# The mixer's list schedule given measured durations, and its weights' low parts always made by VectorE

## The chip, the cores and the metric

One core of one Trainium2 chip. The metric is the device time of one execution in microseconds (us). The engines are named as the profile names them: PE is TensorE's matrix multiplication and PEld its loading of weights, DVE is VectorE, ACT is ScalarE, POOL is GpSimd, and SP is SyncE, which here only issues transfers (DMA).

## What is computed

1024 tokens of width 1024 in float32 go through a layer of two kinds of attention, a layer of attention with forgetting, and a last block: the hybrid mixer, attention over a memory of 256 tokens, and a grouped mixture of experts. The change concerns the mixer and, at its two ends, what is handed over to attention over the memory.

```python
def hybrid_mixer(x, w_in, b_i, b_f, conv_qk, head_norm_g, pool_w, pool_scale, w_out):
    z = x @ w_in
    qk = jax.nn.silu(causal_depthwise_conv(z[..., :2 * M], conv_qk))
    q = qk[..., :M].reshape(B, S, H, dh)
    k = qk[..., M:].reshape(B, S, H, dh)
...
    h = mlstm_chunkwise(q, k, v, i_pre, f_pre)
    mu = h.mean(-1, keepdims=True)
    var = jnp.square(h - mu).mean(-1, keepdims=True)
    h = (h - mu) * lax.rsqrt(var + LN_EPS) * head_norm_g.reshape(H, dh).astype(jnp.float32)
    h = h.reshape(B, S, M) * jax.nn.sigmoid(o_pre.astype(jnp.float32))
    pooled = multiscale_pool(u)
    pm = jnp.einsum('bsgc,gcd->bsgd', pooled, pool_w.astype(jnp.float32))
    pm = pm.reshape(B, S, POOL_WIDTH) * pool_scale.astype(jnp.float32)
    mixed = jnp.concatenate([h, pm], axis=-1).astype(x.dtype)
    return mixed @ w_out
...
        mix = hybrid_mixer(x, ...)
        x = layer_norm(DEEPNORM_ALPHA * x + mix, ln_mix_g[l], ln_mix_b[l])
        xa = memory_cross_attention(x, mem, w_xq[l], w_xkv[l], w_xo[l])
```

H is 4 heads, dh is 128, M is 512; the recurrence of a head runs over chunks, and the pooled part has 4 groups of 128 columns.

## The kernel before

A product of two float32 matrices is made as three products of parts. Each operand is split into a high part, a copy that ACT writes in a type of fewer bits (names in h: `wh`, `fh`), and a low part, the operand minus the high part (`wl`, `fl`). `mm3` (L338 to L343) issues the three matmuls: L340 high by high, L341 and L342 high by low. A weight tile is loaded by SP, ACT makes its high part (L316), and its low part is one subtraction of 128x1024 elements (L318).

The mixer (L1380) has the following stages.

- Eight projections `proj` (L1534), two for each of the four heads, of 48 matmuls each, in two halves and four groups of 6; ACT copies a half out of PSUM (L1548); then the convolution: one first tap (L1556), by DVE or POOL, three more taps by DVE (L1552), a tanh by ACT (L1567), and their product by DVE (L1569).
- Four heads `head` (L1576): masks of exponents (`top`, L1602), their exponentials, scores (L1591) weighed by DVE (L1611), keys turned by PE (L1596), the state's matmuls (L1632) and its updates by DVE (L1642, L1644), the numerator (L1660, L1662, ACT's copy L1667), its statistics (L1672 to L1680), the denominator (L1684 to L1687, a power on POOL L1734, L1735), normalising by ACT, the gate (L1695), a transposition (L1700), high and low parts (L1703, L1707).
- `pool_out` (L1743): four loads of the pooled input (L1752), eight matmuls L1756, their parts (L1759, L1763).
- What is left of the products of weights that depend on the memory alone, which cross-attention needs (`Memory.parts`, L1934). Sixteen groups of the first kind (matmuls L1930, ACT and DVE to tiles `kvw` by L1952, stored to `wkd` by L1962) make the score weights; sixteen of the second kind (L1933, copies L1942 and L1950, stored to `vwd` by L1958) the value weights. They load `x_wq`, `x_wo` (L244) and `kvd` (L1873).
- The eight weights of the out-projection (`m_wo`, L280), and the first half of six of its eight output tiles: `y` loaded with the residual (L1801), four groups of 6 matmuls, and the addition by DVE (L1812).

All that is one list schedule. `class Plan` (L504) takes operations with an engine, a cost in us, a key, what they depend on and what room they take and free (slots of SBUF, banks of PSUM). `run` takes again and again the operation that can start first by these costs, and among equals the lower key; it reckons latencies between engines (L39, 4.0 us for a load). If the engine is a pair such as `("dve", "pool")`, with a pair of costs, it takes the one that would end first. It emits the operations in that order, and each engine then executes its own in order, waiting only for what they need. So costs never change what is done, only the order and, for pairs, the engine.

Behind the list, without a list, follows the rest of the out-projection (L428): 24 matmuls for each remaining half tile, the addition (L422), LayerNorm's statistics (L385, L387), its two passes (L394, L395) with gain and bias loaded at L399, and the store of the tile, which cross-attention loads again as `xl` (L1992), turns, and splits (L2011). Its weights `kw` are loaded from `wkd` (L1987) by SP ahead of LayerNorm's gain and bias for the first ten, and behind for the other six.

Of the kernel before, what the change touches and what calls it, by code (L numbers as in the profile page):

```python
# [14 lines left out]
AF = mybir.ActivationFunctionType  # L15
# [1364 lines left out]
def mixer(k, ft, res, before_out, after_tile):  # L1380
# [58 lines left out]
    act, dve = (lambda n: 0.07 + 0.0008 * n), (lambda n: 0.13 + 0.00092 * n)  # L1439
# [81 lines left out]
    def w_ops(i, key, deps, slot):  # L1521

        def load():
            k.late.discard(i)
            k.w_load(i + 1)
        got, steps = {}, k.w_steps(i)
        loaded[0] = plan.op("sp", 0.1, key, load, [loaded[0], *deps], ["w"])
        d = loaded[1] = plan.op("act", 0.95, key, lambda: next(steps), [loaded[0], loaded[1]], ["sl"] * 2 + ["sl?"] * MX_SPARE[1] if slot else ["wl"])

        def sub(e):  # L1530
            got[0] = steps.send((V, nc.gpsimd)[e])
        return got, plan.op(("dve", "pool"), (1.14, 2.3), key, sub, [d], free=["w"])

    def proj(h, j):  # L1534
# [23 lines left out]
        for half in range(2):  # L1558
            for g in range(4):
                d = plan.op("pe", 1.3, key, lambda half=half, g=g: mm(half, g), [d, e] if half else [d],  # L1560
# [3 lines left out]
        d = plan.op(("dve", "pool"), (0.7, 1.05), key, tap3, [e], ["sl"])  # L1564
        for t in (2, 1, 0):
            d = plan.op("dve", 1.2, key, lambda t=t: tap(t), [d])
        d = plan.op("act", 0.95, key, lambda: nc.scalar.activation(z[0], qk[c], AF.Tanh, scale=0.5), [d])  # L1567
        last_proj.append(e)
        return plan.op("dve", 1.2, key, lambda: V.scalar_tensor_tensor(qk[c], z[0], 1.0, qk[c], op0=OP.add, op1=OP.mult), [d], free=["x"])  # L1569
# [6 lines left out]
    def head(h, ready, begin):  # L1576
# [134 lines left out]
        for b in range(2):  # L1711
            t = chain([("dve", 4 * 0.27, call(top, b), ["sl"] if b == 0 else [], ["x"] if b else []),
                       ("act", 4 * 0.29, call(exps, b))], key, [d])
            s = plan.op("pe", 0.64, key, call(scores, b), ready, ["ps"])
            ev.append(plan.op("dve", 0.6, key, call(weigh, b), [s, t], free=["ps"]))
            kt.append(chain([("pe", 0.44, call(turn_k, b), ["pt"]), ("act", 4 * 0.25, call(scale_k, b), ["sl"] if b == 0 else [], ["pt"])],
# [11 lines left out]
        for i, (a, b) in enumerate(groups):  # L1728
            x = plan.op("pe", (b - a) * 0.23, key, call(num_mm, a, b), [P[(b - 1) // 4], P[0], C[i]], [MX_BANKS[3], "ps"] + ["sl"] * (a == 0),
                        ["sl"] * (4 if b == 8 else 0))  # L1730
            x = plan.op("act", act((b - a) * 129), key, call(num_copy, a, b), [x], [], [MX_BANKS[3]])
            x = plan.op("dve", (b - a) * 0.27, key, call(num_add, a, b), [x, w], free=["ps"])
            N.append(plan.op("dve", (b - a) * 0.28, key, call(stats, a, b), [x]))
        d = chain([("dve", 0.4, den), ("pool", 1.65, lambda: nc.gpsimd.tensor_tensor(rs, rs, k.mhalf[:, :8], op=OP.pow)),  # L1734
                   ("dve", 0.1, lambda: V.scalar_tensor_tensor(nmr, mv[:, :, 0], -1.0, rs, op0=OP.mult, op1=OP.mult))], key, N)  # L1735
        for b in range(2):
            done[b, h] = chain([("act", 1.6, call(normal, b), (), ["sl"] if b else []), ("dve", 0.6, call(gate, b)),
                                ("pe", 0.44, call(turn_p, b), ["pt"], ["sl"] * (2 * b)),
                                ("act", act(512), call(hi, b), ["sl"] * (2 if h % 2 == 0 else 0)),
                                ("dve", 0.6, call(lo, b), (), ["pt"])], key, [d] + ([done[b, h - 1]] if h % 2 else []))  # L1740
    done = {}

    def pool_out():  # L1743
# [21 lines left out]
        for g in range(4):  # L1765
            key = MX_KEYS[0] + g / 10
            d = plan.op("sp", 0.1, key, lambda g=g: load(g), [d], ["x"] + ["sl"] * (g == 0))
            for half in range(2):
                d = plan.op("pe", 0.86, key, lambda g=g, half=half: mm(g, half), [d], [MX_BANKS[4]],
                            (["x"] if half else []) + (["sl"] if half and g == 3 else []))  # L1770
                e = plan.op("act", 0.5, key, lambda g=g, half=half: hi(g, half), [d], ["sl"] * (2 if g % 2 == 0 else 0))
                d = done[half, 4 + g] = plan.op("dve", 0.62, key, lambda g=g, half=half: lo(g, half), [e], free=[MX_BANKS[4]])
# [1166 lines left out]
```

## Time and profile before

| what | before |
|---|---|
| median of 3 runs | 2295.5 us (2295.07 to 2298.74) |
| the profiled execution | 2301.81 us, span 2300.0 us |
| its mean granted clock of TensorE | 0.988 |
| PE busy | 2211.1 us, 96% of the span, 12164 instructions |
| DVE busy | 1184.4 us, 51%, 2892 instructions |
| ACT busy | 960.0 us, 42%, 2018 instructions |
| POOL busy | 452.6 us, 20%, 620 instructions |
| DMA | 282.06 MB, mean 123 GB/s |

The profiled execution is one run of its own, and its 2301.81 us contain the span and 1.8 us around it. The share of an engine's busy time is a mean over all stages. The mixer's list covers some 190 us before 1642 us of the span.

### The profile page before, as it was taken

What the parts mean: (1) busy time and instruction counts of PE and PEld (TensorE: products, weight loads), DVE (VectorE), ACT (ScalarE), POOL (GpSimd) and SP (SyncE); (2) the same over time, 40 slices, a digit from 0 to 9 for tenths busy, and PEclk for the clock granted to TensorE, in tenths of its full rate; (3) what the DMA queues carried; (4) which work ended last, traced back from release to release, by engine and by line L of the source; (5) the groups of instructions that cost most, each with busy time, mean ns of one, the idle gap of its engine ahead of it and who ended that gap; (6) DMA issues with size and microseconds to landing.
All of it is one profiled execution on the core that took longest, in us unless ns stands there. A gap on an engine that the chain in (4) does not pass through costs nothing.

```text
span 2300.0 us, 32867 instructions
## 1 busy us (share of the span) xinstructions
PE 2211.1 (96%) x12164; PEld 1757.5 (76%) x12164; DVE 1184.4 (51%) x2892; ACT 960.0 (42%) x2018; POOL 452.6 (20%) x620
## 2 busy tenths in 40 slices
PE   7999999999999999999999999999899999899797
PEld 7888778888877777777788789787577888666564
DVE  6322678834344443444344332687445637766544
ACT  5322667823344444444442221355202122557453
POOL 2000455400122222222310010121001102222121
PEclk9999999999999999999999999999999999999898
DMA  4112221233222211221254221326656124778774
GB/s 165 37 48 99 81 58 38 75 118 104 75 69 72 63 55 60 74 60 56 83 174 147 103 91 47 106 69 216 233 220 259 69 106 176 263 235 293 226 216 165
DMA packets 96515, 282.06 MB, mean 123 GB/s; under 512 B 11980, under 2 KB 25036, under 8 KB 96352
## 3 DMA queue, kind: packets, MB, share of 16 engines
q1 hardware_dynamic: 75616, 225.32, 28.4%
q0 software_dynamic: 6624, 24.12, 4.4%
q10 hardware_dynamic: 14112, 30.48, 4.2%
q8 instruction: 97, 1.59, 0.3%
q14 instruction: 66, 0.54, 0.1%
HBM read 202.73 MB, written 65.62 MB: 117 GB/s over the span
## 4 chain that ended last, share of the span: by engine, by line
PE 85%; DVE 6%; DMA 4%; ACT 3%; issue 2%; SPq 0%; POOL 0%; ACTq 0%; POOLq 0%; DVEq 0%
PE pd L340 15%; PE pd L342 15%; PE pd L341 15%; PE ps L340 4%; PE po L644 4%; PE ps L342 4%; PE ps L341 4%; PE ps L595 3%; PE pt L622 3%; PE pd L2538 2%; PE pd L1902 2%; PE ps L990 2%; PE po L1033 1%; PE pt L1019 1%; PE ps L2562 1%
## 5 line engine op out<-in xcount | busy, mean ns | idle before, releaser
L340 PE MATMUL pd<-fh,wh 128*128 128x512 f32 x880 | 353.5, 402 | 0.6 <-DVE st L1246 0.3
L342 PE MATMUL pd<-fh,wl 128*128 128x512 f32 x880 | 347.9, 395 | 0.5 <-DVE wl L318 0.5
L341 PE MATMUL pd<-fl,wh 128*128 128x512 f32 x880 | 347.4, 395 | 0.0
L340 PE MATMUL pd<-wh,fh 128*128 128x258 f32 (+3 forms) x616 | 203.2, 330 | 2.4 <-DVE n L1436 2.4
L342 PE MATMUL pd<-wh,fl 128*128 128x258 f32 (+3 forms) x616 | 200.9, 326 | 0.0
L341 PE MATMUL pd<-wl,fh 128*128 128x258 f32 (+3 forms) x616 | 200.8, 326 | 0.0
L340 PEld LDWEIGHTS pd<-fh,wh 128*128 128x128 f32 x880 | 165.2, 188 | 43.0 <-issue 7.1
L342 PEld LDWEIGHTS pd<-fh,wl 128*128 128x128 f32 x880 | 165.2, 188 | 40.1 <-issue 2.3
L341 PEld LDWEIGHTS pd<-fl,wh 128*128 128x128 f32 x880 | 165.5, 188 | 34.9 <-issue 0.2
L318 DVE TENSOR_TENSOR wl<-w,wh 128x1024 fp32r<-128x1024 f32 (+5 forms) x92 | 106.8, 1166 | 138.3 <-ACT wh L316 138.3
L316 ACT CAST wh<-w 128x1024 fp32r<-128x1024 f32 (+5 forms) x99 | 97.3, 989 | 139.3 <-PE pd L341 108.2
L630 ACT COPY PT<-pt 128x512 f32<-128x512 f32 (+2 forms) x192 | 86.4, 478 | 139.9 <-PE pt L622 139.4
L609 POOL TENSOR_SCALAR P<-P,rinv 128x256 f32<-128x256 f32 (+7 forms) x128 | 96.1, 751 | 192.3 <-DVE rinv L608 163.3
L606 ACT ACTIVATE P<-P,m 128x256 f32<-128x256 f32 (+7 forms) x128 | 99.6, 778 | 76.7 <-DVE m L600 75.8
L340 PEld LDWEIGHTS pd<-wh,fh 128*128 128x128 f32 x616 | 116.4, 189 | 14.2 <-DVE n L1436 2.8
L341 PEld LDWEIGHTS pd<-wl,fh 128*128 128x128 f32 x616 | 116.3, 189 | 10.6 <-issue 1.0
L342 PEld LDWEIGHTS pd<-wh,fl 128*128 128x128 f32 x616 | 116.3, 189 | 10.2 <-issue 0.2
L1309 POOL TENSOR_TENSOR dm<-lcb,mask 128x128 f32<-128x128 f32 x128 | 60.7, 474 | 282.4 <-DVE m L600 226.3
L595 PE MATMUL ps<-st,st 128*128 128x512 f32 (+3 forms) x384 | 106.9, 372 | 1.2 <-DMA st<-st 0.8
L644 PE MATMUL po<-PT,V 128*64 128x256 f32 (+1 forms) x640 | 96.4, 373 | 0.0
L2420 DVE TENSOR_TENSOR ml<-mw,mh 128x1024 fp32r<-128x1024 f32 x66 | 80.1, 1226 | 29.8 <-ACT mh L2417 15.4
L622 PE MATMUL pt<-ident,P 128*128 128x128 f32 x576 | 88.7, 276 | 2.6 <-POOL P L609 2.4
(513 smaller groups left out, 4721.9 us busy)
## 6 DMA issues: line engine op xcount, KB each, us to landing
mw<-w_moe SPq DMA_DIRECT2D x70, 512.0 KB
w<-o_wc SPq DMA_DIRECT2D x30, 512.0 KB
w<-w_moe SPq DMA_DIRECT2D x26, 512.0 KB
xr<-xs SPq DMA_DIRECT2D x18, 512.0 KB
s<-x_wkv SPq DMA_DIRECT2D x16, 512.0 KB
lcb<-dn SPq DMA_DIRECT2D x16, 512.0 KB
st<-st ACTq DMA_DIRECT2D x64, 128.0 KB
wkd<-kvw SPq DMA_DIRECT2D x32, 256.0 KB
```

The lines of the kernel that those rows point to most:

```text
L316: nc.scalar.copy(hi[:, :n], raw[:, :n])
L318: (eng or nc.vector).tensor_sub(lo[:, :n], raw[:, :n], hi[:, :n].bitcast(F32))
L340: first = mm(out, lhs[0], rhs[0], start=start, stop=False)
L341: mm(out, lhs[0], rhs[1], start=False, stop=False)
L342: mm(out, lhs[1], rhs[0], start=False, stop=stop)
L595: ins = nc.tensor.matmul(ps[:, :m], l, r, start=t == 0, stop=t == len(passes) - 1)
L606: nc.scalar.activation(sb[:, :w], sb[:, :w], AF.Exp, bias=acc, scale=-1.0, accum_out=sm)
L609: nc.gpsimd.tensor_scalar(sb[:, :w], sb[:, :w], ri, 0.0, op0=OP.mult, op1=OP.add)
L622: ins = nc.tensor.transpose(pt[:, j * 128:(j + 1) * 128], p[:, (c + j) * 128:(c + j + 1) * 128], k.ident)
L630: nc.scalar.copy(dst, src)
L644: st["V", n + i] = nc.tensor.matmul(o[a * 64:(a + 1) * 64, cols], val(a, j), PT[i // 2, a, j // 4][:, j % 4, n0:], start=j == 0, stop=j == ...
L2420: nc.vector.tensor_sub(W[c][1], raw[c], W[c][0].bitcast(F32))
```

## The change

Every cost of the mixer's list is replaced by another number; so are the costs of the memory steps. The low part of a weight is no longer given to DVE or POOL, whichever would end first, but always to DVE. Nothing else is changed: the operations, the tiles and the room are the same. These lines show the kinds of edits; the other costs change in the same way.

```diff
-    act, dve = (lambda n: 0.07 + 0.0008 * n), (lambda n: 0.13 + 0.00092 * n)
+    act, dve = (lambda n: 0.155 + 0.00085 * n), (lambda n: 0.155 + 0.00104 * n)
...
-        def sub(e):
-            got[0] = steps.send((V, nc.gpsimd)[e])
-        return got, plan.op(("dve", "pool"), (1.14, 2.3), key, sub, [d], free=["w"])
+        def sub():
+            got[0] = steps.send(V)
+        return got, plan.op("dve", 1.23, key, sub, [d], free=["w"])
...
-                d = plan.op("pe", 1.3, key, lambda half=half, g=g: mm(half, g), [d, e] if half else [d],
+                d = plan.op("pe", 1.4, key, lambda half=half, g=g: mm(half, g), [d, e] if half else [d],
...
-        d = plan.op(("dve", "pool"), (0.7, 1.05), key, tap3, [e], ["sl"])
+        d = plan.op(("dve", "pool"), (0.75, 1.13), key, tap3, [e], ["sl"])
...
-            t = chain([("dve", 4 * 0.27, call(top, b), ["sl"] if b == 0 else [], ["x"] if b else []),
+            t = chain([("dve", 4 * 0.49, call(top, b), ["sl"] if b == 0 else [], ["x"] if b else []),
...
-            x = plan.op("pe", (b - a) * 0.23, key, call(num_mm, a, b), [P[(b - 1) // 4], P[0], C[i]], [MX_BANKS[3], "ps"] + ["sl"] * (a == 0),
+            x = plan.op("pe", (b - a) * 0.45, key, call(num_mm, a, b), [P[(b - 1) // 4], P[0], C[i]], [MX_BANKS[3], "ps"] + ["sl"] * (a == 0),
...
-                @add("act", 0.3 if kind else 0.5)
+                @add("act", 0.37 if kind else 0.6)
...
-                @add("dve", 0.35 if kind else 0.6)
+                @add("dve", 0.42 if kind else 0.68)
```

In all, the seven low parts that POOL made leave it, and the first taps on POOL become four of eight instead of two; no instruction is added or removed. Three places show how the order moves. In the names, the number behind a name only tells tiles apart.

The first place is DVE in the fourth head, from the weighing of its scores on. L318 rows are the low parts of weights of the out-projection, L1642 and L1644 the head's state, L1952 the memory's score weights, L1763 the pooled part. Before:

```order
L1569 SCALAR_TENSOR_TENSOR qk_15025<-z_14902,qk_15025 128x1024
L1952 SCALAR_TENSOR_TENSOR kvw_15048<-ps_15017,kvw_15048 128x512
L1952 SCALAR_TENSOR_TENSOR kvw_15051<-po_15042,kvw_15051 128x512
L1763 SCALAR_TENSOR_TENSOR fl_15095<-ps_15056,psc_13831,fh_15094 128x512
L318 TENSOR_TENSOR wl_15104<-w_15035,wh_15103 128x1024
L1611 SCALAR_TENSOR_TENSOR e_15061<-ps_15108,e_15061 128x512
L1952 SCALAR_TENSOR_TENSOR kvw_15138<-ps_15066,kvw_15138 128x512
L1611 SCALAR_TENSOR_TENSOR e_15061<-ps_15133,e_15061 128x512
L1642 COPY C_15164<-pd_15144 128x129
L1644 SCALAR_TENSOR_TENSOR C_15164<-C_15164,n_12840,pd_15144 128x129 x2
L1626 TENSOR_TENSOR n_12840<-n_12840 128x8
L1627 TENSOR_TENSOR n_12840<-n_12840 128x8
```

Now:

```order
L1611 SCALAR_TENSOR_TENSOR e_15025<-ps_15061,e_15025 128x512
L318 TENSOR_TENSOR wl_15059<-w_14995,wh_15058 128x1024
L1763 SCALAR_TENSOR_TENSOR fl_15067<-ps_15018,psc_13831,fh_15066 128x512
L1611 SCALAR_TENSOR_TENSOR e_15025<-ps_15089,e_15025 128x512
L1626 TENSOR_TENSOR n_12840<-n_12840 128x8
L1627 TENSOR_TENSOR n_12840<-n_12840 128x8
L318 TENSOR_TENSOR wl_15075<-w_14997,wh_15074 128x1024
L1952 SCALAR_TENSOR_TENSOR kvw_15005<-po_14981,kvw_15005 128x512
L1642 COPY C_15132<-pd_15116 128x129
L1644 SCALAR_TENSOR_TENSOR C_15132<-C_15132,n_12840,pd_15116 128x129 x2
L1719 TENSOR_SCALAR n_12840<-n_12840 128x8
L318 TENSOR_TENSOR wl_15145<-w_15100,wh_15144 128x1024
```

Three low parts now stand in DVE's queue from the first weighing to the middle of the state's updates, where one stood ahead of the weighing; two more of that stretch were POOL's. Of three of the memory's L1952 there, one is left.

The second place is SP at the boundary to cross-attention, the last rows ahead of the weights `kw`: stores `vwd` of the memory's value weights, loads of `x_wo` (named s) and `kvd`, and residuals `xr`. Before:

```order
L1801 DMA y_15474<-xs_5683 128x1024
L1958 DMA vwd<-vwo_15472 128x512
L244 DMA s_15504<-x_wo 128x1024
L1873 DMA kv_15506<-kvd 128x2x256
L244 DMA s_15531<-x_wo 128x1024
L1958 DMA vwd<-vwo_15634 128x512
L1958 DMA vwd<-vwo_15641 128x512
L1958 DMA vwd<-vwo_15648 128x512
L1958 DMA vwd<-vwo_15655 128x512
L1826 DMA xr_15660<-xs_5683 128x1024
L1826 DMA xr_15662<-xs_5683 128x1024
L1987 DMA kw_15664<-wkd 128x1024
```

Now:

```order
L1958 DMA vwd<-vwo_15614 128x512
L244 DMA s_15621<-x_wo 128x1024
L1873 DMA kv_15623<-kvd 128x2x256
L1958 DMA vwd<-vwo_15625 128x512
L1958 DMA vwd<-vwo_15635 128x512
L1958 DMA vwd<-vwo_15639 128x512
L244 DMA s_15643<-x_wo 128x1024
L1958 DMA vwd<-vwo_15651 128x512
L1958 DMA vwd<-vwo_15655 128x512
L1826 DMA xr_15660<-xs_5683 128x1024
L1826 DMA xr_15662<-xs_5683 128x1024
L1987 DMA kw_15664<-wkd 128x1024
```

Behind the last `y` load, nine stores of value weights instead of five now stand ahead of the `kw` loads (the first four of the nine are not shown), with a further load of `kvd` and one more of `x_wo`; on PE, eight of sixteen groups L1933 instead of four stand inside the out-projection, the last of them 164 matmuls ahead of its end.

The third place is DVE in the LayerNorm behind the out-projection: the first pass (L394) and the second (L395) of the six tiles `y`, among the additions (L422) of later tiles, `xr` being tile 6. Before:

```order
L387 BN_AGGR mv_15828<-bn_15825 128x2
L394 SCALAR_TENSOR_TENSOR y_15420<-y_15420,mv_15717,s_15684 128x1024
L394 SCALAR_TENSOR_TENSOR y_15422<-y_15422,mv_15754,s_15684 128x1024
L394 SCALAR_TENSOR_TENSOR y_15424<-y_15424,mv_15791,s_15684 128x1024
L394 SCALAR_TENSOR_TENSOR y_15454<-y_15454,mv_15828,s_15684 128x1024
L422 SCALAR_TENSOR_TENSOR y_15470<-y_15470,pd_15836 128x512
L395 SCALAR_TENSOR_TENSOR y_15420<-y_15420,rstd_15719,s_15686 128x1024
L395 SCALAR_TENSOR_TENSOR y_15422<-y_15422,rstd_15756,s_15686 128x1024
L395 SCALAR_TENSOR_TENSOR y_15424<-y_15424,rstd_15793,s_15686 128x1024
L395 SCALAR_TENSOR_TENSOR y_15454<-y_15454,rstd_15830,s_15686 128x1024
L385 BN_STATS bn_15862<-y_15470 128x6
L422 SCALAR_TENSOR_TENSOR y_15474<-y_15474,pd_15885 128x512
```

Now:

```order
L422 SCALAR_TENSOR_TENSOR xr_15660<-xr_15660,ps_15922 128x512
L385 BN_STATS bn_15974<-xr_15660 128x6
L394 SCALAR_TENSOR_TENSOR y_15388<-y_15388,mv_15717,s_15684 128x1024
L394 SCALAR_TENSOR_TENSOR y_15390<-y_15390,mv_15754,s_15684 128x1024
L394 SCALAR_TENSOR_TENSOR y_15392<-y_15392,mv_15791,s_15684 128x1024
L394 SCALAR_TENSOR_TENSOR y_15419<-y_15419,mv_15828,s_15684 128x1024
L394 SCALAR_TENSOR_TENSOR y_15428<-y_15428,mv_15865,s_15684 128x1024
L394 SCALAR_TENSOR_TENSOR y_15432<-y_15432,mv_15914,s_15684 128x1024
L395 SCALAR_TENSOR_TENSOR y_15388<-y_15388,rstd_15719,s_15686 128x1024
L395 SCALAR_TENSOR_TENSOR y_15390<-y_15390,rstd_15756,s_15686 128x1024
L422 SCALAR_TENSOR_TENSOR xr_15660<-xr_15660,pd_15948 128x512
L395 SCALAR_TENSOR_TENSOR y_15392<-y_15392,rstd_15793,s_15686 128x1024
```

Before, four tiles' first passes stood ahead of the fifth tile's addition, and their second passes behind it. Now six first passes stand in one block behind the addition of the first half of tile 6.

## Rows read from the trace of the kernel before

**Rows 1.** Windows: us, then each engine's busy us (instructions), PE's granted clock, DMA share, GB/s.
```profile
1448.00:1580.60 132.60, 131.38 (x700) 111.69 (x699) 99.66 (x243) 60.57 (x135) 25.05 (x10) 1.00 0.32 100
1580.60:1642.60 62.00, 51.30 (x204) 31.91 (x203) 42.12 (x97) 32.51 (x67) 7.42 (x3) 0.97 0.93 328
1642.60:1738.60 96.00, 96.00 (x400) 74.73 (x399) 41.59 (x58) 2.55 (x6) 9.26 (x17) 1.00 0.53 195
1738.60:1790.00 51.40, 49.87 (x242) 40.42 (x241) 29.97 (x49) 21.11 (x46) 0.74 (x2) 1.00 0.63 237
1650.00:1670.00 20.00, 20.00 (x86) 15.95 (x85) 4.90 (x7) 0.69 (x1) 0.00 (x0) 1.00 0.01 2
```

**Rows 2.** Waits of PE, 1448 to 1643: what it waited for, us in all, times, longest.
```profile
PE ps L1930 <- DMA kv<-kvd: 3.0, 1, 3.0
...
PE pt L1700 <- DVE p L1695: 0.9, 1, 0.9
...
PE ps L1591 <- DVE qk L1569: 0.3, 1, 0.3
```

**Rows 3.** Timeline of POOL: start, us, engine, line, operation, tiles, count, idle time before and what ended it.
```profile
1511.90 3.38 POOL L318 TENSOR_TENSOR wl<-w,wh 128x1024 fp32r<-128x1024 f32 x1 [4.99 <-PE pt L1700]
...
1596.30 2.37 POOL L318 TENSOR_TENSOR wl<-w,wh 128x1024 fp32r<-128x1024 f32 x1 [7.55 <-ACT wh L316]
```

**Rows 4.** Timeline of DVE, 1460 to 1645.
```profile
1462.60 5.93 DVE L1552 SCALAR_TENSOR_TENSOR qk<-z,conv,qk 128x1023 f32<-128x1023 f32 x3
...
1512.97 0.68 DVE L1707 TENSOR_TENSOR fl<-pt,fh 128x512 fp32r<-128x512 f32 x1
...
1582.63 3.91 DVE L1552 SCALAR_TENSOR_TENSOR qk<-z,conv,qk 128x1023 f32<-128x1023 f32 x3
1586.46 2.44 DVE L1602 CUSTOM_DVE_ANT_0 e<-ab,mask,n 128x128 f32<-128x128 f32 x1
...
1588.83 0.34 DVE L1602 CUSTOM_DVE_ANT_0 e<-ab,mask,n 128x128 f32<-128x128 f32 x1
...
1630.53 1.23 DVE L318 TENSOR_TENSOR wl<-w,wh 128x1024 fp32r<-128x1024 f32 x1 [1.42 <-ACT wh L316]
```

**Rows 5.** Timeline of PE from the last projection matmul to the out-projection's resumption.
```profile
1580.55 0.60 PE L1700 MATMUL pt<-ident,p 128*128 128x128 f32 x4
1580.98 1.89 PE L1930 MATMUL ps<-kv,s 128*128 128x256 f32 x8
1582.71 1.89 PE L1930 MATMUL po<-kv,s 128*128 128x256 f32 x8
...
1640.37 1.13 PE L1756 MATMUL ps<-pl,s 128*128 128x512 f32 x2 [2.02 <-DMA pl<-pooled]
...
1642.64 0.79 PE L340 MATMUL pd<-wh,fh 128*128 128x512 f32 x1
```

**Rows 6.** Timeline of SP: DMA issues of the tail and the boundary.
```profile
1631.45 0.32 SPq L1752 DMA_DIRECT2D pl<-pooled  x1
...
1689.15 13.34 SPq L1987 DMA_DIRECT2D kw<-wkd  x10
1702.58 0.38 SPq L399 DMA_DIRECT2D s<-ln_mix_g  x1
...
1724.31 1.03 SPq L1992 DMA_DIRECT2D xl<-xs  x2
```

**Rows 7.** Timeline of DVE, 1660 to 1750.
```profile
1710.13 4.87 DVE L394 SCALAR_TENSOR_TENSOR y<-y,mv,s 128x1024 f32<-128x1024 f32 x4 [3.28 <-DMA s<-ln_mix_g]
...
1715.52 4.86 DVE L395 SCALAR_TENSOR_TENSOR y<-y,rstd,s 128x1024 f32<-128x1024 f32 x4
...
1721.92 0.69 DVE L422 SCALAR_TENSOR_TENSOR xr<-xr,ps 128x512 f32<-128x512 f32 x1 [0.35 <-PE ps L342]
...
1739.97 0.67 DVE L2011 TENSOR_TENSOR xl<-pt,xh 128x512 fp32r<-128x512 f32 x1
```

**Rows 8.** The tile kw: operations with durations in ns and first and last start.
```profile
L340 PE MATMUL ps<-kw,xh x16: 391/394/477, 1741.8 to 1752.3; 128*128 128x512 f32 x16
```

More of the change, by code (lines that the diff above doesn't have):

```diff
@@ L1711, in head @@
         for b in range(2):
-            t = chain([("dve", 4 * 0.27, call(top, b), ["sl"] if b == 0 else [], ["x"] if b else []),
[L1713 to L1716, printed above, removed]
+            t = chain([("dve", 4 * 0.49, call(top, b), ["sl"] if b == 0 else [], ["x"] if b else []),
+                       ("act", 4 * 0.39, call(exps, b))], key, [d])
+            s = plan.op("pe", 0.9, key, call(scores, b), ready, ["ps"])
+            ev.append(plan.op("dve", 0.68, key, call(weigh, b), [s, t], free=["ps"]))
+            kt.append(chain([("pe", 0.46, call(turn_k, b), ["pt"]), ("act", 4 * 0.37, call(scale_k, b), ["sl"] if b == 0 else [], ["pt"])],
                             key, ready + [gates]))
@@ L1721, in head @@
         for a, b in ((0, 3), (3, 6), (6, 7)):
-            C.append(chain([("pe", (b - a) * 0.11, call(state_mm, a, b), [MX_BANKS[2]] + ["sl"] * (a == 0), ["sl"] if b == 7 else []),
-                            ("dve", (b - a) * 0.27, call(state, a, b), [], [MX_BANKS[2]])], key,
+            C.append(chain([("pe", (b - a) * 0.224, call(state_mm, a, b), [MX_BANKS[2]] + ["sl"] * (a == 0), ["sl"] if b == 7 else []),
+                            ("dve", (b - a) * 0.345, call(state, a, b), [], [MX_BANKS[2]])], key,
                            [kt[(b - 1) // 4], kt[0]] + C[-1:]))
@@ L1770, in pool_out @@
                             (["x"] if half else []) + (["sl"] if half and g == 3 else []))
-                e = plan.op("act", 0.5, key, lambda g=g, half=half: hi(g, half), [d], ["sl"] * (2 if g % 2 == 0 else 0))
-                d = done[half, 4 + g] = plan.op("dve", 0.62, key, lambda g=g, half=half: lo(g, half), [e], free=[MX_BANKS[4]])
+                e = plan.op("act", 0.68, key, lambda g=g, half=half: hi(g, half), [d], ["sl"] * (2 if g % 2 == 0 else 0))
+                d = done[half, 4 + g] = plan.op("dve", 0.75, key, lambda g=g, half=half: lo(g, half), [e], free=[MX_BANKS[4]])
     for h in range(4):
@@ L1816, in mixer @@
         for j, g in enumerate(MO_ORDER[:4]):
-            d = plan.op("pe", 1.3, key, lambda i=i, g=g: out_part(i, g), [d, y, ready[g], done[0, 2 * g], done[0, 2 * g + 1]],
+            d = plan.op("pe", 1.4, key, lambda i=i, g=g: out_part(i, g), [d, y, ready[g], done[0, 2 * g], done[0, 2 * g + 1]],
                         [bank] if j == 0 else [])
-        plan.op("dve", 0.62, key, lambda i=i: out_add(i), [d], free=[bank])
+        plan.op("dve", 0.69, key, lambda i=i: out_add(i), [d], free=[bank])
     with k.tc.manual_schedule(engines=SW_MAN):
```

18 lines of the change are left out of this document (9 added, 9 removed).

## The prediction

> **What bounds the kernel now.** Read first the windows by stage around the mixer's planned part [rows 1]. PE is busy 131.38 of 132.60 us while the eight projections run, 51.30 of 62.00 in the tail behind them, 96.00 of 96.00 in the rest of the out-projection, and 49.87 of 51.40 where cross-attention begins. So only two stretches can give anything: the tail, where PE idles 10.7 us with its transfers at a share of 0.93 and 328 GB/s, and the boundary. Where PE is full, only work that enters or leaves counts. The PE waits of the planned part come second [rows 2]: the longest, 3.0 us, ends on the load of kvd, and on VectorE (DVE) end 0.9 and 0.3 us while the projections run. Then each engine's timeline: POOL for what a low part costs there [rows 3], DVE for what it costs others [rows 4], PE for where the projections end and the out-projection resumes [rows 5], SP for the loads behind it [rows 6], and DVE and PE at the boundary [rows 7, 8].
>
> Call P the last projection matmul (ended by 1580.55), R the resumption of the out-projection (1642.64) [rows 5], and E its end (1738.60). The list decides P, R and what PE still has to do behind R.
>
> **The low parts.** Seven of sixteen go from POOL, where one alone takes 2.37 us [rows 3], to DVE, at 1.23 us [rows 4]: 7 x 1.23 = 8.6 us more. While POOL made them, DVE's own instructions were stretched in six of seven cases: three taps took 5.93 us instead of 3.91 in the first, one exponent's mask 2.44 instead of 0.34 in the last [rows 4]. The six together add about 11.5 us (six times 1.5 to 2.2). An instruction that reads PSUM was not stretched (L1707, 0.68 us from 1512.97, beside POOL's low part of 1511.90 to 1515.28) [rows 3, 4]. So DVE gets some 3 us lighter; two first taps (L1556) that move to POOL as well are counted at nothing, since no PE wait of the tail ends on them. On the path lie only the 0.9 and 0.3 us that PE waited for DVE [rows 2]: **-1.2 us**, bounds -1.2 and 0; I take all of it, and +0.5 for new waits of the same kind, since low parts now stand in the queue ahead of the gate (L1695).
>
> The Trainium skill, "SBUF — State Buffer", section "SBUF: two separate sides", says that the pair of ports that VectorE and GpSimd share is locked for a whole instruction, and that the other engine waits it out (VectorE where it reads two operands from SBUF). By that rule all seven low parts would give DVE back up to their whole length; the rows give less than that for each, and since neither lies on the path the sum is the same by both.
>
> **P.** The new order has one group of memory weights (L1930) fewer ahead of the last projection matmul and one transposition of head 2 (L1700) fewer. A group is a row of eight matmuls, and the next group starts 1.73 us on, from 1580.98 to 1582.71; the transposition before it holds PE 0.43 us, from 1580.55 to 1580.98 [rows 5]. So P moves by -1.73 - 0.43 - 1.2 + 0.5 = **-2.9 us**.
>
> **The tail, P to R, 62.1 us before.** PE's work in it was 51.3; one L1930 and one L1700 enter (+2.2), four groups of L1933, which I price as L1930's, leave for behind R (12 of 16 stood ahead of it, now 8), 4 x 1.73 = 6.9. That leaves 46.6, so PE is not what ends it: transfers are. R needs the last of the four pooled loads, issued at 1631.45 and waited for until 1640.37 [rows 5, 6], so 8.9 us in flight. In the new order 1.75 MB fewer stand ahead of it: two x_wo loads of 128x1024 in float32 (0.5 MB each), two vwd stores and, since P, one wkd store (0.25 MB each). Two bounds. If the transfers alone set it, 1.75 MB / 328 GB/s = 5.3 us are gained. If the chain of head 3 sets it, less: its product (L1569) has four masks fewer ahead of it (4 x 0.27), no stretch (2.1), but a gate and a low part of 0.69 and 0.68 more, so the scores come some 1.6 us earlier behind P; from there the third low part stands in DVE's queue and waits for its load, I put 2.2 us, and everything behind it, the head's state above all, stands too; slots come free later, and of the 1.6 us little but the time in flight remains. I take 1.6 earlier in issue and 2.1 us shorter in flight (8.9 to 6.8, by the fewer stores ahead), **-3.7 us**, between -5.3 and 0. R: -2.9 - 3.7 = -6.6.
>
> **R to E.** 16 half tiles of 24 matmuls, 6 already done, are 15.75 halves. 86 matmuls take 20.00 us [rows 1], so one takes 0.233 and a half 5.58: 87.9; four L1933 groups add 6.9, and cross-attention's first transpositions the rest of the 96.0. Now eight groups stand there: **+6.9 us**. PE is full, so all of it counts. E: -6.6 + 6.9 = +0.3. What the tail gains is what was carried out of it.
>
> **The boundary.** The last vwd store can go only when the last L1933 is done, and the 16 kw loads stand behind it on SP. Before, SP came to the kw at 1689.15, E - 49.5 [rows 6]. Now the last L1933 stands 164 matmuls ahead of E, 164 x 0.233 = 38.1 us, so the kw start at about E - 36. LayerNorm's gain and bias stand behind the first ten. They were issued 13.4 us behind the first kw, and DVE's first normalising (L394) began 7.5 us after the gain's issue at 1702.58, E - 28.5 [rows 6, 7]. In the new DVE order six L394 stand in one block, behind the first half of tile 6, which ended its add at 1722.61, E - 16 [rows 7]; so the block starts at about E - 15.3. Six L394 at 1.217 (four took 4.87) and the first L395, 8.5 us, make tile 0 ready at E - 6.8. It is stored and read back (xl); before, 7.6 us lay between its normalising (1715.52 + 4.86 / 4 for its L395) and SP's xl at 1724.31, with six kw loads between, so 0 to 7.6; I take 2.9, because the kw are gone by then. DVE meanwhile has five more L395, the adds and statistics of tiles 6 and 7, and reaches cross-attention's first low part (L2011, 1739.97 before, E + 1.4) at about E + 3.3, and one L394 later the second one, until some E + 5.9. The first score matmuls came at 1741.8, E + 3.2 [rows 8], and now come at E + 6.4: **+3.2 us**. Bounds: -1.5, all the idle time of that stretch [rows 1], and +7, if gain and bias land only at E - 11.6.
>
> One row speaks for hiding part of it: from 1650 to 1670 the DMA share was 0.01 [rows 1], so the four stores that leave the tail find free engines there.
>
> **Sum.** -2.9 - 3.7 + 6.9 + 3.2 = **+3.5 us**. Against the profiled execution, 2301.8 us, that is 2305.3. It stood 6.3 us above the median of the three runs, 2295.5; I carry the difference over: **2299.0 us**. About 0.2%, 4.6 us, is what a measurement of this kernel tells from no change, so 2290.9 and 2300.1 are the borders, and the forecast lies inside, near the upper.
>
> **Rivals.**
> Faster (A). The loads no longer stand behind slots in the tail. 20.3 MB went through it (62.0 us at 328 GB/s); less 1.75 are 18.6, and at a share of 1.00 in place of 0.93 (353 GB/s) they need 52.7 us. Then P to R shrinks by 9.4 instead of 3.7, E stands at -2.9 - 9.4 + 6.9 = -5.4, and with the boundary hidden the time is 2290.1. For it: the wait of 3.0 us for kvd [rows 2] is for a load issued after two m_wo; m_wo 0 and 1 are now earlier, and DVE is lighter. Against it: the pooled loads still wait for one another's buffers, so the share need not rise.
>
> The Trainium skill, "Perfetto Trace Analysis", section "Optimizing Scalar/DVE Operations", says that moving work between VectorE and GpSimd might not help, since they share a port; that speaks for A, and against having had the low parts on POOL at all. The rows agree in the stretched taps, but PE waited only 1.2 us for them, and by rule or row the gain on the path is that.
>
> Slower (B). DVE takes its queue in order. On POOL a low part could wait for its load at no cost: the one at 1596.30 had stood 7.55 us for ScalarE's high part, which waits for the load [rows 3]; on DVE one stood 1.42 us [rows 4]. Now three stand among head 3's state updates. If the third waits as long as POOL did, 7.55 instead of 2.2, the head is 5.3 us later, R and E with it: +3.5 + 5.3 = +8.8, 2304.3. It decides from the point where the load of the third m_wo lets DVE wait over 2.2 us. For: m_wo 2 is issued behind x_wq and kvd. Against: 1.75 MB fewer are in its way.
>
> No change (C). The tail gives what it is charged later (+0.3) and the boundary is hidden in DVE's slack: 2295.8. That the change does nothing is excluded, since the order shows seven low parts gone from POOL.
>
> **How the numbers follow.** Forecast 0.47, its own range 2293 to 2304 (the tail's -5.3 to 0 and the boundary's -1.5 to +7 around the sum, which seldom meet), of which 0.32 lie within 0.2%, 0.13 above and 0.02 below. A 0.25, faster. B 0.20, slower. C 0.08, within. Faster 0.27, same 0.40, slower 0.33. The range reaches to 2288.5, A with another 1.6 us, and to 2307.0, B with the boundary at most of its upper bound.
>
> **What would show it.** Right: no L318 on POOL and three taps near 3.9 us everywhere; the last projection matmul some 3 us earlier; R at about 1636; eight groups L1933 behind R; the kw loads from about 1702, a block of six L394 near 1723 and the first score matmuls 6 us behind E. Wrong: PE idle in the tail far below 11.8 us (A) or above 15 with DVE standing before an L318 (B), or score matmuls within 3 us of E (C or A).

## The result and the profile after

The change makes the kernel slower: 2311.9 us (median of 6 runs, 2309.9 to 2314.7) against 2297.6 us of the kernel before (6 runs, 2295.1 to 2301.3). The ratio is 1.0061, 95% interval 1.0051 to 1.0071, so 14.0 us, interval 12 to 16. The forecast was 2299.0, range 2288.5 to 2307.0, so the measured time lies above the range.

To see where the time went, both traces are laid on the same point, the first copy of a projection out of PSUM (L1548; 1454.2 us before, 1452.4 now). All times in this table are behind that copy, but the last column:

| | before | after | difference | forecast |
|---|---|---|---|---|
| P, end of the last projection matmul | 126.3 | 122.4 | -3.9 | -2.9 |
| R, the out-projection resumes | 188.4 | 185.0 | P to R: +0.5 | -3.7 |
| E, its last matmul ends | 284.2 | 288.4 | R to E: +7.6 | +6.9 |
| first score matmul of cross-attention | 287.5 | 299.2 | from E: +7.4 | +3.2 |
| last maximum of cross-attention (L2063) | 477.1 | 489.9 | from there: +1.2 | 0 |
| sum | | | +12.8 | +3.5 |

12.8 of the 14 us are in this stretch. The windows of the kernel after by stage, which answer to [rows 1] (us, then each engine's busy us with its instructions, in the order PE, PEld, DVE, ACT, POOL, then the granted clock, DMA share, GB/s):

```profile
1448.00:1574.84 126.84, 126.84 (x680) 108.29 (x679) 90.92 (x239) 55.86 (x124) 10.34 (x7) 1.00 0.37 119
1574.84:1637.44 62.60, 52.16 (x202) 34.90 (x200) 42.91 (x99) 34.73 (x73) 2.57 (x2) 0.89 0.71 248
1637.44:1740.86 103.42, 103.29 (x414) 77.27 (x412) 39.48 (x57) 4.36 (x10) 5.56 (x15) 1.00 0.47 177
1740.86:1792.30 51.44, 44.45 (x197) 35.60 (x197) 27.13 (x42) 17.07 (x37) 3.31 (x4) 0.90 0.72 280
1576.00:1588.00 12.00, 8.17 (x38) 6.58 (x37) 11.45 (x28) 10.70 (x25) 0.00 (x0) 0.81 0.01 4
1620.00:1625.00 5.00, 4.80 (x7) 2.03 (x8) 1.31 (x4) 0.59 (x2) 0.00 (x0) 0.66 1.05 391
1625.00:1630.00 5.00, 4.03 (x10) 1.44 (x8) 2.30 (x4) 2.75 (x5) 0.00 (x0) 1.00 1.03 379
1630.00:1637.40 7.40, 7.32 (x19) 3.62 (x20) 1.94 (x6) 1.12 (x3) 0.00 (x0) 1.00 1.03 409
```

The first four rows are the projections, the tail, the rest of the out-projection, and the boundary; the last four are pieces of the tail. PE has no idle time left in the projections. In the tail it is busy 52.16 of 62.60 us, as much as before (51.30 of 62.00), although four groups L1933 have left it; the clock row tells part of that, 0.89 instead of 0.97. The mean DMA share of the tail has fallen from 0.93 to 0.71, but it is a mean of two parts: from 1576 to 1588 the transfers stood still, at a share of 0.01, and from 1588 to R it is 0.89, from 1620 on 1.03 to 1.05. The tail moved 15.5 MB (62.6 us at 248 GB/s), where it had moved 20.3. And 51.4 us of the boundary, from E on, hold 44.45 us of matmuls instead of 49.87.

PE's timeline after, which answers to [rows 5, 8]:

```profile
1574.61 0.39 PE L342 MATMUL pd<-fh,wl 128*128 128x512 f32 x1
...
1581.02 0.66 PE L1700 MATMUL pt<-ident,p 128*128 128x128 f32 x4 [1.71 <-DVE p L1695]
1582.71 0.66 PE L1700 MATMUL pt<-ident,p 128*128 128x128 f32 x4 [1.04 <-DVE p L1695]
1584.45 2.08 PE L1591 MATMUL ps<-qk,qk 128*128 128x128 f32 x8 [1.08 <-DVE qk L1569]
...
1636.88 1.12 PE L1756 MATMUL ps<-pl,s 128*128 128x512 f32 x2
1637.44 0.79 PE L340 MATMUL pd<-wh,fh 128*128 128x512 f32 x1
...
1740.63 0.40 PE L342 MATMUL pd<-wh,fl 128*128 128x512 f32 x1
1746.50 1.97 PE L2003 MATMUL pt<-ident,xl 128*128 128x128 f32 x8 [5.47 <-DMA xl<-xs]
...
1751.58 0.78 PE L340 MATMUL ps<-kw,xh 128*128 128x512 f32 x1
```

The projections end at 1574.84. Then PE stands before head 2's gate (L1700, twice) and before head 3's first scores (L1591, 2.08 us). The out-projection resumes at 1637.44 and ends at 1740.86; the first transposition of cross-attention waits 5.47 us for the load of xl, and the first score matmul comes at 1751.58, 10.7 us behind E, where it came 3.3 us behind it. SP's timeline, which answers to [rows 6]:

```profile
1567.19 0.90 SPq L280 DMA_DIRECT2D w<-m_wo  x2
...
1568.68 0.69 SPq L1873 DMA_DIRECT2D kv<-kvd  x1
1588.41 4.01 SPq L280 DMA_DIRECT2D w<-m_wo  x2
...
1630.88 0.45 SPq L1752 DMA_DIRECT2D pl<-pooled  x1
...
1702.17 2.04 SPq L1958 DMA_DIRECT2D vwd<-vwo  x2
...
1705.27 8.21 SPq L1987 DMA_DIRECT2D kw<-wkd  x10
1714.40 0.33 SPq L399 DMA_DIRECT2D s<-ln_mix_g  x1
...
1716.98 15.81 SPq L1987 DMA_DIRECT2D kw<-wkd  x6
1739.99 1.54 SPq L1992 DMA_DIRECT2D xl<-xs  x2
```

SP issued kvd at 1568.68 and then stood until 1588.41 at the third m_wo load, whose buffer the first low part frees; that is the idle DMA of 1576 to 1588. So this load went at P + 13.6. Before, it had gone at P + 8.2, behind a first low part that GpSimd made from P + 5.7 on. SP's and GpSimd's rows before:

```profile
1588.78 0.33 SPq L280 DMA_DIRECT2D w<-m_wo  x1
```

```profile
1586.25 2.50 POOL L318 TENSOR_TENSOR wl<-w,wh 128x1024 fp32r<-128x1024 f32 x1 [11.76 <-ACT wh L316]
```

SP stayed late: the fourth pooled load, which the last pooled matmuls ahead of R need, was issued at 1630.88, P + 56.0, where it had been P + 50.9 (1631.45 in [rows 6]). It was faster from there: its matmuls (L1756) began 6.0 us behind the issue instead of 8.9. At the boundary the last two vwd stores went at 1702.17, the kw from 1705.27, the gains at 1714.40, and xl at 1739.99, 7.2 us behind SP's last kw issue (1716.98 + 15.81), when the store of that tile had landed. VectorE and ScalarE there, which answer to [rows 4, 7] (ACTq is ScalarE's DMA queue):

```profile
1584.04 1.05 ACT L316 CAST wh<-w 128x1024 fp32r<-128x1024 f32 x1
...
1734.18 7.39 ACTq L2899 DMA_DIRECT2D xs<-y  x6
```

```profile
1587.17 1.22 DVE L318 TENSOR_TENSOR wl<-w,wh 128x1024 fp32r<-128x1024 f32 x1
...
1594.20 1.23 DVE L318 TENSOR_TENSOR wl<-w,wh 128x1024 fp32r<-128x1024 f32 x1 [0.53 <-ACT wh L316]
...
1725.71 7.25 DVE L394 SCALAR_TENSOR_TENSOR y<-y,mv,s 128x1024 f32<-128x1024 f32 x6
1732.88 2.47 DVE L395 SCALAR_TENSOR_TENSOR y<-y,rstd,s 128x1024 f32<-128x1024 f32 x2
...
1748.27 0.69 DVE L2011 TENSOR_TENSOR xl<-pt,xh 128x512 fp32r<-128x512 f32 x1 [4.49 <-ACT xh L2006]
```

The first low part came 12.3 us behind P, for ScalarE had made its high part only at 1584.04, and it and VectorE had head 2's gate and head 3's taps and masks in their queues ahead of it. The six L394 began at 1725.71, E - 15.2, and the first L395 ended at 1734.15, E - 6.7: both as forecast. The store of the first tile was issued at 1734.18, the load of xl 5.8 us later, and PE could start 6.5 us behind that.

### The profile page after: what moved, and what is told of

Same layout as the page of the kernel before. It is cut to its first block, busy times and chain, and to the rows that moved or that the text cites. A ratio compares the mean times of both kernels' runs of the same rounds, so it can differ in the third digit from the quotient of the medians.

```text
span 2308.1 us, 32884 instructions
## 1 busy us (share of the span) xinstructions
PE 2216.8 (96%) x12164; PEld 1761.8 (76%) x12164; DVE 1180.3 (51%) x2897; ACT 959.4 (42%) x2018; POOL 432.9 (19%) x615
## 5 line engine op out<-in xcount | busy, mean ns | idle before, releaser
L318 DVE TENSOR_TENSOR wl<-w,wh 128x1024 fp32r<-128x1024 f32 (+5 forms) x99 | 115.3, 1169 | 137.4 <-ACT wh L316 133.5
L2420 DVE TENSOR_TENSOR ml<-mw,mh 128x1024 fp32r<-128x1024 f32 x66 | 80.1, 1227 | 30.0 <-ACT mh L2417 15.5
```

The costliest lines, as they stand in the source:

```text
L318: (eng or nc.vector).tensor_sub(lo[:, :n], raw[:, :n], hi[:, :n].bitcast(F32))
L2420: nc.vector.tensor_sub(W[c][1], raw[c], W[c][0].bitcast(F32))
```

## The experiments

All ratios are to the kernel before, run beside each. The change itself is at 1.0061. A row of a run names the lines of that run's own kernel, so the same code can stand a few lines higher or lower there.

| run | ratio | 95% interval | P to R, us | E to first score, us |
|---|---|---|---|---|
| low parts only | 1.0063 | 1.0047 to 1.0080 | 62.6 | 10.5 |
| costs only | 1.0108 | 1.0091 to 1.0125 | 64.6 | 17.7 |
| gains first | 1.0058 | 1.0042 to 1.0075 | 62.5 | 8.6 |
| memory first | 1.0021 | 1.0011 to 1.0030 | 64.2 | 3.3 |
| fill | 1.0045 | 1.0030 to 1.0059 | 61.2 | 9.9 |
| two low parts early | 1.0079 | 1.0061 to 1.0097 | 65.6 | 10.5 |
| xl before the last kw | 1.0017 | 1.0007 to 1.0027 | 60.5 | 3.4 |
| early and memory first | 1.0030 | 1.0017 to 1.0043 | 67.7 | 3.3 |
| three on GpSimd | 1.0057 | 1.0040 to 1.0074 | 62.6 | 10.0 |
| before, loads reordered | 1.0000 | 0.9990 to 1.0009 | 60.7 | 3.3 |
| fill and xl first | 1.0019 | 1.0010 to 1.0028 | 59.8 | 3.3 |

The kernel before has 62.1 and 3.3. In the stretch P to R the last run of before with reordered loads is the same program as before, and took 60.7; so a difference under 2 us there is not told apart from chance by one trace. In the two runs with the memory first, both last pairs of pooled matmuls stand ahead of R, not one, which puts 0.9 us of work into their tails.

**The two halves of the change.** First its second half alone:

```diff
 (the kernel before, with its costs)
...
-        return got, plan.op(("dve", "pool"), (1.14, 2.3), key, sub, [d], free=["w"])
+        return got, plan.op("dve", 1.14, key, sub, [d], free=["w"])
```

> The costs of the kernel before, with the low parts always on VectorE. Its order is like the change's: eight groups L1933 behind the resumption, the last one 164 matmuls ahead of the out-projection's end, six L394 in one block. My theory (the loss sits at the boundary, where the last store of value weights, the kw loads, LayerNorm's gains and so the xl load come late, and in a tail that is not shortened) expects 7 to 14 us over before, with the first score matmul 9 to 11 us behind the out-projection's end. Rival (the new costs are what hurts, the low parts are harmless): within 3 us of before.

It took 1.0063, the first score 10.5 us behind E: as my theory had it, and a little more than its 14 us allowed at the upper end (14.5). Then its first half alone (most costs, not every one: PE's costs of the pooled matmuls, the transpositions behind the gate and the memory steps are the same in both kernels):

```diff
 (the change, with its costs)
...
-        return got, plan.op("dve", 1.23, key, sub, [d], free=["w"])
+        return got, plan.op(("dve", "pool"), (1.23, 2.4), key, sub, [d], free=["w"])
```

> The change's costs, with the low parts on VectorE or GpSimd, whichever would end first (1.23 and 2.4). Eight of them are on GpSimd. The last L1933 stands even later in the out-projection than in the change, and the six L394 stand behind the first half of tile 7. My theory expects the boundary to cost at least as much as in the change: first score matmul 10 to 16 us behind the out-projection's end, 7 to 14 us over before in all. Rival (low parts in VectorE's queue are the cause): within 3 us of before.

1.0108, 24.8 us, with the first score 17.7 us behind E: both more than my theory's upper ends, and no rival's 3 us. Here 122 matmuls stand behind the last L1933, where the change has 164 and before had 223, and PE waited 13.2 us for xl. In the tail it waited 5.6 us for the last pooled load. So neither half is harmless, and the two do not add. What the three lists have in common is that value weights are left for late in the out-projection.

**The boundary.** Gains ahead of the kw loads:

```diff
+    gb = [k.bcast(A["ln_mix_g"], D), k.bcast(A["ln_mix_b"], D)]
     before_out()
-    gb = [k.bcast(A["ln_mix_g"], D), k.bcast(A["ln_mix_b"], D)]
```

> The change, with LayerNorm's gain and bias loaded ahead of the kw loads instead of behind the first ten. Nothing of the tail moves. VectorE's L394 then stand four tiles early, one half tile behind the tiles' own additions. My theory expects tile 0 to be stored some 8 us earlier, the xl load right behind the last kw load, the first score matmul 3 to 5 us behind the out-projection's end instead of 10.7, and 5 to 7 us less than the change. Rival (the boundary's loss follows from kw loads and their traffic, not from LayerNorm): under 2 us.

A miss for my theory, and the rival's number: 8.6 us from E to the first score, 2.1 us less than the change, and 1.0058 in all, 0.7 us less. VectorE's first L394 did come at 1709.54 and the first tile's store was issued at 1718.52, 20.5 us ahead of E instead of 6.7; but xl stood behind the kw loads. SP's timeline and PE's of that run:

```profile
1703.49 0.38 SPq L399 DMA_DIRECT2D s<-ln_mix_g  x1
...
1704.39 29.85 SPq L1987 DMA_DIRECT2D kw<-wkd  x16
1734.29 1.61 SPq L1992 DMA_DIRECT2D xl<-xs  x2
```

```profile
1742.40 1.97 PE L2003 MATMUL pt<-ident,xl 128*128 128x128 f32 x8 [3.17 <-DMA xl<-xs]
...
1747.65 0.78 PE L340 MATMUL ps<-kw,xh 128*128 128x512 f32 x1
```

The 16 kw loads hold SP for 29.85 us, xl is issued at 1734.29, and 8.1 us later, at 1742.40, PE can start. So my account by LayerNorm alone was wrong, and the second account was that the kw loads and their 8 MB stand in xl's way. It was put to the test with this edit on top of the last one:

```diff
-        elif i == 5:
-            self.weights(range(5, 8))
...
         self.load(1)
+        self.weights(range(5, 8))
```

> The change, with LayerNorm's gain and bias ahead of the kw loads, and the last six kw loads behind the first two xl loads. Theory (at the boundary it is the 16 kw loads, 8 MB, behind the late value stores, that keep xl away; in the run with the gains alone ahead they still did): xl lands before the out-projection ends, first score matmul 3 to 4.5 us behind its end, 5 to 7 us less than the change. Rival (what is left there is not the order of the loads): 8 us or more behind the end, as with the gains alone.

SP's timeline and PE's of that run:

```profile
1704.68 9.65 SPq L1986 DMA_DIRECT2D kw<-wkd  x10
1723.02 5.89 SPq L1991 DMA_DIRECT2D xl<-xs  x2
1728.97 6.59 SPq L1986 DMA_DIRECT2D kw<-wkd  x6
```

```profile
1739.37 1.04 PE L2002 MATMUL pt<-ident,xl 128*128 128x128 f32 x8
...
1742.71 0.47 PE L340 MATMUL ps<-kw,xh 128*128 128x512 f32 x1
```

xl goes at 1723.02, does not let PE wait, and the first score matmul comes 3.4 us behind E. The ratio is 1.0017: 10.1 us of the change's 14.0 are back, more than the 5 to 7 expected. In the trace the scores also keep their clock (see the next section), and the tail is 2 us shorter than the change's. The same order of loads in the kernel before is the control:

> The kernel before, with the load order of the earlier experiment at the boundary: gain and bias ahead, the last six kw loads behind the first two xl loads. Theory (the order of the loads only matters where the last value store is late): within 2 us of before, first score matmul 3 to 4 us behind the out-projection's end as before. Rival (that order is worth something by itself, and the gain over the change was that): 3 us or more faster than before.

1.0000, and 3.3 us from E: the order of the loads is worth nothing where the last value store is early. The other way round, the last L1933 is brought forward and the loads stay as they are:

```diff
-MX_KEYS = (5, 100, 0, 5, 3.9)
+MX_KEYS = (5, 100, 0, 5, 101)
```

> The change, with the list's key of the planned output tiles behind the memory steps' key, so that the last L1933 stands 244 matmuls ahead of the out-projection's end instead of 164. The tail up to the resumption is the change's own. My theory expects the kw loads 15 to 18 us earlier, the first score matmul 3 to 5 us behind the out-projection's end, and 5 to 7 us less than the change. Rival (the loss is in the tail alone): within 2 us of the change.

The kw loads began at 1688.58, 54.2 us ahead of E instead of 35.6, the first score came 3.3 us behind E, 1.0021: 9.2 us less than the change, again more than expected. Both ways out of the same wait give back about the same, and the control gives back nothing, so the loss at the boundary is shown.

**The tail.** Here the theories did worse. The slow clock first. The 5 us windows of the change where it was lost, columns as above:

```profile
1580.00:1585.00 5.00, 1.86 (x10) 1.39 (x11) 5.00 (x18) 5.00 (x12) 0.00 (x0) 0.85 0.00 0
1585.00:1590.00 5.00, 5.00 (x25) 5.00 (x24) 3.57 (x8) 4.57 (x14) 0.00 (x0) 0.50 0.17 19
```

PE was busy 1.86 of 5.00 us, and in the next window the granted clock was 0.50, the lower of its two levels (1.2 GHz); eight score matmuls took 2.08 us where they had taken 1.06.

```diff
         def turn_p(b):
             pt = B["t", b] = k.pst()
+            for c in range((16, 9)[b] if h == 2 else 0):
+                nc.tensor.transpose(pt[:, at(c % 4)], k.ident, k.ident)
...
             s4 = B["s", b] = k.pss()
+            for c in range(9 if (h, b) == (3, 0) else 0):
+                nc.tensor.transpose(s4[:, at(c % 4)], k.ident, k.ident)
```

> The change, with 34 transpositions of the identity that nobody reads, put where TensorE stood behind the projections: 16 and 9 ahead of the two transpositions of head 2 (L1700), 9 ahead of head 3's first scores. Nothing else moves. Theory (TensorE stood there for 3.8 us, and the matmuls behind it then ran at a granted clock of 0.5): from the last projection matmul to the resumption 2.5 to 4 us less than the change's 62.6, eight score matmuls near 1.06 us instead of 2.08, 2 to 4 us less in all. Rival (the tail is set by its transfers, and slow matmuls only fill waits): the same time from the projections to the resumption within 1 us.

The tail's window and PE's timeline there:

```profile
1573.99:1635.22 61.23, 50.94 (x235) 34.03 (x234) 42.51 (x99) 34.62 (x73) 2.57 (x2) 1.00 0.72 254
```

```profile
1578.30 1.91 PE L1702 MATMUL pt<-ident 128*128 128x128 f32 x16
...
1580.66 1.15 PE L1702 MATMUL pt<-ident 128*128 128x128 f32 x9
...
1582.36 1.15 PE L1591 MATMUL ps<-ident 128*128 128x128 f32 x9
1583.60 1.16 PE L1593 MATMUL ps<-qk,qk 128*128 128x128 f32 x8
```

The clock was 1.00 all through the tail, the scores took 1.16 us, and the tail 61.2 us: 1.4 less than the change, between the theory's 2.5 and the rival's 1, and within what one trace does not tell from chance. The whole took 1.0045, 3.7 us less, but its interval and the change's meet. With the loads mended, the filling was worth nothing that can be told:

> The run with xl before the last kw loads and the 34 unread transpositions together. Theory (the two losses are apart from each other: the slow clock behind the projections, and the loads at the boundary): tail 60 to 61.5 us with a granted clock of 1.00, first score matmul 3 to 4 us behind the out-projection's end, and 1 to 3.5 us less than with the loads alone, so 2298 to 2301, about as before. Rival (the clock's loss is covered by waits where the run happens to keep its clock, as in the run with the loads alone): within 1 us of that run.

1.0019 against 1.0017 without it, tail 59.8 against 60.5: the rival. But both tails had a mean granted clock of 0.97, not the 1.00 that I expected with the filling, so this pair says little of the clock. In the kernels with the change's order in the tail it took 62.5 to 62.6 us at 0.89 to 0.92, 60.5 and 59.8 at 0.97, and 61.2 at 1.00. So the slow clock costs some 1 to 3 us of the tail, as far as single traces tell, and most of the 5.5 us by which the slow matmuls are longer (52.2 against 46.7, below) stands where PE would have waited.

Of the 50.94 us of PE work in that filled tail the 34 transpositions are 4.2 (1.91 + 1.15 + 1.15), so the tail's own work at full clock is 46.7; the forecast had 46.6. What it had wrong was the rest of the tail: 61.2 - 46.7 = 14.5, not 11.8.

Then SP's stand of 19.0 us before the third m_wo load. The load, high part and low part of each of the first two weights (`early`) are moved up in the list's output, behind the copy of the last projection (`anchor`); the lines that fill the two names are left out here:

```diff
...
+            rest = [i for i in out if i not in self.early]
+            at = rest.index(self.anchor) + 1
+            out = rest[:at] + self.early + rest[at:]
         for i in out:
             ops[i][3]()
```

> The change, with the high and low parts of the out-projection's first two weights moved up on ScalarE and VectorE, from behind head 2's gate and head 3's masks to right behind the last projection's copy. Theory (the DMA engines stood idle for 13 us because SP stood at the third weight's load, which waits for the first low part): the third weight's load at 4 to 6 us behind the last projection matmul instead of 13.6, the idle stretch gone for its first 8 us, and the tail 1 to 4 us shorter, though head 3's scores come 2 to 2.5 us later and the next store of score weights still waits for VectorE. Rival (the tail hangs on head 3's chain): 1 to 3 us longer.

SP's timeline and PE's of that run:

```profile
1576.93 1.47 SPq L280 DMA_DIRECT2D w<-m_wo  x2
1578.45 15.96 SPq L1970 DMA_DIRECT2D wkd<-kvw  x2
```

```profile
1583.32 1.11 PE L1705 MATMUL pt<-ident,p 128*128 128x128 f32 x4 [4.93 <-DVE p L1700]
```

The third m_wo load went 3 us behind P. But SP stood nearly all of these 15.96 us at the second of the two stores, a wkd whose VectorE part (L1952 in the change) stands in that queue behind head 3's work, the gate came later (PE's first wait 4.93 us), and the tail grew by 3.0 us. That is the rival's number. The theory was not put to the test, though: SP's stand was moved, not removed, and from 1578.45 to 1594.40 the DMA share was 0.22. With the memory first it is the same (tail 67.7):

> The run with the memory first and the two early low parts together. If both theories hold the gains add: 1 to 4 us less than the memory first alone, 2298 to 2302, about as before. Rival: as the memory first alone or 1 to 3 us more.

1.0030, 2 us more than the memory first alone, as the rival had it, though the intervals meet; the tails of the two traces differ by 3.5 us. Last, the engine of the low parts, with every queue otherwise as in the change:

```diff
-            got[0] = steps.send(V)
+            got[0] = steps.send(nc.gpsimd if i in [k.mo[c] for c in MO_ORDER[:3]] else V)
```

> The change with every queue in its own order, except that the first three low parts of the out-projection's weights are carried out by GpSimd, not by VectorE (three L318 fewer in VectorE's queue behind the projections, three more in GpSimd's). Theory (the tail hangs on VectorE's queue, where those three stand ahead of head 3's state): the state's updates 1 to 3 us earlier, and from the projections to the resumption 1 to 3 us less than the change's 62.6. Rival (the engine of the low parts does not matter, only where the list puts things): within 1 us.

1.0057, tail 62.6: no difference, the rival, though GpSimd needed 4.85 us for two low parts and VectorE was rid of three. Head 3's first states (L1644) came 17.6 us behind P instead of 18.0. The third m_wo load went only 0.7 us earlier (P + 12.9), for the first low part still waited for ScalarE's high part, from P + 9.2 on (before: P + 4.6). With the queues as they stand in the change, which engine makes the low parts does not matter in this tail.

What sets the 62.6 us is thus narrowed down, not settled: not the engine of the low parts, not the third m_wo load alone, and the clock by 1 to 3 us. The transfers are not ruled out. In the seven kernels that end the tail in the change's order (the change, gains first, fill, two low parts early, xl before the last kw, three on GpSimd, fill and xl first), R came 6.4 to 7.4 us behind the issue of the fourth pooled load, while that issue went from P + 52.8 to P + 58.9. So R goes with that load. What makes SP come to it late is open. Candidates are SP's stands for buffers and copies, and the chains through ACT and DVE behind them: head 2's gate, head 3's taps and scores, and the copies that free PSUM for the next memory step. No run here shortened one of these alone.

No version beats the kernel before. The best of the change's line, with the xl loads ahead of the last kw loads, is 4 us above it.

## Why the prediction was wrong

- **P** (-2.9): right in kind, -3.9. PE's waits for DVE in the projections are gone altogether (126.84 of 126.84), and one L1930 and one transposition stand behind. The new waits ahead of the gate, for which I had put +0.5 here, came in the tail: 1.71 and 1.04 us (L1700).
- **R to E** (+6.9): right, +7.6. The other 0.7 us stand from 1638.30 to 1639.91 in the change, where four matmuls of the out-projection hold PE 0.34 to 0.48 us each instead of 0.23 while it waits for the parts of the last pooled pair (L1759, L1763), which now stands directly ahead of R. One pooled pair stands behind R in both traces (1652.76 before, 1648.25 now) and changes nothing; it, and not cross-attention's transpositions, belongs to the rest of the 96.0 us before.
- **The tail** (-3.7): failed, +0.5, outside my bounds of -5.3 to 0. The step that failed is the issue of the fourth pooled load: I took it 1.6 us earlier behind P, from head 3's earlier scores, and it came 5.2 us later (P + 56.0). The time in flight went the way that I had, and further (8.9, forecast 6.8, measured 6.0), and R stood 0.6 us behind the load's matmuls instead of 2.3: +5.2 - 2.9 - 1.7 is the +0.5. Fewer bytes (4.8 MB fewer in the whole tail) gained nothing: SP stood at the third m_wo load until P + 13.6, where it had stood until P + 8.2, and the transfers stood with it (share 0.04 from P to 1588). I had priced a stand of VectorE (2.2 us) and none of SP. What keeps SP late from there to the pooled load stays open. PE's work was right (46.7 at full clock), but I had not priced a fall of the clock, though the trace before had 0.97 in its tail; in the change PE was busy 52.2 us and idle 10.4.
- **The boundary** (+3.2): the mechanism was right, the size was not, +7.4. Start of the six L394 (E - 15.3; measured E - 15.2), tile 0 ready (E - 6.8; E - 6.7) and VectorE free for L2011 (E + 3.3; E + 2.9) were as forecast. The mis-sized term is the way of the tile out and back: 2.9 us from ready to xl's issue, measured 5.8, and after that I let the load be there by E + 3.3; it took 6.5 us from issue to PE's start, so E + 5.6. VectorE then stood 4.49 us for it. I had taken 2.9 "because the kw are gone by then", and they were not: SP had issued the last one, but from 1734.20 to 1740.00 the DMA share was 0.99. Where they were gone, in the costs-only run (share 0.01 from 1745.00 to 1749.30), the store took 2.7 us to xl's issue. The row to take was the 7.6 us that lay between a tile's L395 and xl's issue before.
- **Behind it** (0): +1.2. Standing for xl, PE lost its clock (0.90 over the boundary's 51.4 us, 1.00 before) and the first score matmul took 0.78 us instead of 0.48; with xl in time this is gone (189.8 us from the first score to the last maximum, 189.6 before, 190.7 in the change).
- **The rivals.** B came out on the right side, by the wrong mechanism: VectorE stood only 0.53 us before the third low part (1594.20), not over 2.2 (it did stand 2.20 us before a later one, at 1628.45, where PE then lost 1.0 for a copy of value weights). The stand was SP's, before a load whose buffer VectorE had not freed. A's premise did not come about: the share of the transfers fell to 0.71 instead of rising to 1.00. C had the boundary hidden, and it cost 7.4.
- **The port rule.** With no low part on GpSimd three taps take 3.92 us at 1460.78, and 5.93 us for three are gone. As forecast that gave PE nothing in the tail. The Trainium skill, "SBUF — State Buffer", section "SBUF: two separate sides", has it that the engine that starts first holds the shared ports for its whole instruction and the other waits. The trace before agrees better than I had read it: one low part on GpSimd (1462.81 to 1466.13, 3.32 us instead of 2.37) began beside a running tap, and of the three taps only the next one was long (1463.92 to 1467.21), and it ended 1.1 us behind the low part. So each waited the other out.

The Trainium skill, "Perfetto Trace Analysis", section "Optimizing Scalar/DVE Operations", has it that moving work between VectorE and GpSimd might not help. The run with three low parts on GpSimd agrees: 1.0057 against 1.0061.

## What to carry to other kernels

New durations in a list schedule, even measured ones, need not make a better schedule where the list does not know what comes behind it: here it moved four groups of work, 6.9 us by the forecast's price, past its own end, and with it the stores that the next stage's loads stand behind. Before trusting such a change, find the last store that another stage's loads queue behind, and count its distance from the stage's end; here 223, 164 and 122 matmuls gave waits for xl of 0, 5.5 and 13.2 us. And give a tile that goes out and comes back its measured time, here 12.3 us from store to use beside other transfers (7.9 in the run where the other transfers were done). And read a mean DMA share in its parts: 0.71 was 0.04 for 13 us and 0.89 behind them.

## What the runs showed that was not expected

- A tile of 0.5 MB stored by ScalarE's queue and loaded again needed 5.8 us to the load's issue and 6.5 more to PE's start, 12.3 in all, beside other transfers (share 0.99 and 1.00). With the other transfers done (costs only) it needed 2.7 and 5.2.
- The same program took 62.1 and 60.7 us from P to R, and the change's tail 62.6, 62.5 and 60.5 in three kernels with the same order there, with mean granted clocks of 0.89, 0.92 and 0.97.
- Slow matmuls cost little where PE waits anyway: a tail at clock 1.00 was only 1.4 us shorter than one at 0.89, though PE's own work in them differs by 5.5 us (52.2 against 46.7).
